# A hybrid RWKV-7 and convolution decoder step on one core: gates, LayerNorm, next input and first loads in another order, and three of each pair's four channel sums as products of two parts

## Chip, core and metric

One Trainium2 chip, one core. The metric is the device time of one execution in microseconds (us). Engines: TensorE (PE in the rows, PEld its weight loads), VectorE (DVE), ScalarE (ACT), GpSimd (POOL) and SyncE (SP), whose queue issues most of the DMAs; ScalarE can issue DMAs too.

## What is computed

One layer, over a prompt of 2048 tokens and 8 single sample tokens, all in float32, with 1024 channels, 16 heads of 64, and a convolution branch of 512 channels. Cut to what matters here:

```python
h = rms_norm(x, norm_pre_g)
proj = h @ w_in                     # r k v z | two lora inputs | conv-glu | z_conv | gate_r gate_c
ps = ps + (ps_prev - ps) * mu_shift # token shift of the first columns
kk = kk * rsqrt(sum(kk * kk, -1) + 1e-12)          # per head (sum 1)
y_w, wkv_new = wkv7_scan(...)                      # recurrence per head
mu = mean(y_w, -1); var = mean(square(y_w - mu), -1)   # GroupNorm per head (sums 2 and 3)
bonus = sum(rh * kh * r_k, -1) * vh                # per head (sum 4)
o_r = (y_gn + bonus) * silu(z_r)
c = causal depthwise conv of width 31 of the GLU
o_c = silu(LayerNorm(c)) * silu(z_c)
merged = sigmoid(g_r) * (o_r @ w_branch_r) + sigmoid(g_c) * (o_c @ w_branch_c)
y = x + rms_norm(merged @ w_out, norm_post_g)
```

## The kernel before

**Tiles and blocks.** Channels lie on the 128 partitions, tokens along the free dimension. The prompt is cut into 4 blocks of 512 tokens (`for b in range(NB)`, L1167). In a block, the 8 pairs of heads are worked on one after the other (`for j in range(HP)`, L1177). `unit_in` (L486) projects r, k, v and z of a pair into "raw" tiles, `unit_a` (L503) makes decay, keys and the triangular solve of the eight 64-token chunks, `unit_b` (L657) runs the recurrence and GroupNorm and leaves the pair's output in an "orr" tile. `unit_in` runs two pairs ahead. Between the pairs, `fill` (L1132) puts in other projections by the strings FILL0 to FILL2 (L299): "u" is `glu` (L743), "n" is `conv_norm` (L762), the LayerNorm of the convolution branch, "z" and "Z" are `conv_gate`, a digit is `gate` (L998), which computes two of the 16 gate tiles and stores them in DRAM. After the pairs come `stage_a` (L376) with the next block's input, its first projections, then eight `merge` steps (L1020), which load the gates again, and `stage_out` (L1045). In the last block `final_states` (L1146) stands ahead of the merge.

**Products.** `gemm` (L307) multiplies float32 values split in two parts: `split` (L137) has ScalarE copy the value into a float32r tile (the high part) and VectorE subtract that from the value (the low part); three products of parts make one product (PASSES, L305), all recorded at L113. The sums over a head's 64 channels go another way: `stat` (L362) is one float32 product of 512 columns with a constant matrix, `ones_b` (ones in two blocks of 64) or `cent` (identity minus the mean). The trace has two records for each such product. A pair has four of them: of the squared keys (L536, stays as it is), of the bonus (L654, input R, output multiplied by V into "keep"), and two of GroupNorm in the "gt" tile (L711 with `cent` into "py", L713 with `ones_b` into "pc").

**Order.** All is unrolled. The framework lays out each engine's instructions ahead of the run by a list scheduler: every instruction has a priority (its place in the program; `tc.high_priority(n)` puts it n places earlier, `later(n)` (L158) n places later), and among what is ready by planned times the earliest goes first. On the chip each engine's queue runs in that fixed order and waits where a semaphore says so. Tiles of one name share a number of buffers (BUFS, L71: x 2, raw 8, orr 8, w 5, ht 8, tmp 4; aw, gd and pz 1 each; "pg" has 3 PSUM banks). `pull` (L725) deals out the convolution's taps on VectorE, the tile "et".

**Lines that the steps touch.** `gate` computes Exp, Ln, Exp on ScalarE in an "x" tile and stores both halves from SP (L1011); `merge` loads them from SP (L1027, L1028) into "x"; `stage_a` loads the next block's input from SP (L385) into "x", scales it on VectorE and splits it into "ht"; `final_states` collects the state in "x"; `stage_first` (L390) loads sample rows on ScalarE's queue and the first block's input on SP's, into "orr" and "x"; L237 loads the convolution weights. P (L662) has a tile "pz"; `pr` (L581), where the solve keeps its products, is in "gd".

Of the kernel before, what the change touches and what calls it, by code (L numbers as in the profile page):

```python
# [18 lines left out]
LN = 60  # L19
# [7 lines left out]
def rwkv7_conformer_step(  # L27
# [91 lines left out]
    def f32(ap):  # L119
        return ap.bitcast(F32)  # L120
# [48 lines left out]
    def cmem(shape, v, name):  # L169
        t = const.tile(shape, F32, name=name)  # L170
        nc.gpsimd.memset(t, v)
        return t
# [5 lines left out]
    ones_b = cmem([128, 128], 0.0, "ones_b")  # L178
# [22 lines left out]
    cent = const.tile([128, 128], F32, name="cent")  # L201
# [3 lines left out]
    stt(cent, ones_b, -1.0 / 64, ident, ALU.mult, ALU.add)  # L205
# [25 lines left out]
    for name, _, n in _VECS:  # L231
# [5 lines left out]
    nc.scalar.dma_start(out=crow[0:NTAP * CT, :], in_=conv_w)  # L237
    ps = pa()
    nc.tensor.transpose(out=ps[:, 0:nrow], in_=rows[0:nrow, :], identity=ident[0:nrow, 0:nrow])
    nc.tensor.transpose(out=ps[:, 128:128 + NTAP * CT], in_=crow[0:NTAP * CT, :],  # L240
                        identity=ident[0:NTAP * CT, 0:NTAP * CT])
    prm = const.tile([128, nrow], F32, name="prm")
    cw = const.tile([128, NTAP * CT], F32, name="cw")
    vcp(prm, ps[:, 0:nrow])
    vcp(cw, ps[:, 128:128 + NTAP * CT])
# [120 lines left out]


# [8 lines left out]
    def stage_a(b):  # L376
# [3 lines left out]
        for k2 in range(KT // 2):  # L380
            xt = new([128, 2, BS], "x")
            for i in range(2):
                with tc.high_priority(HPA):
                    kt = 2 * k2 + i
                    nc.sync.dma_start(out=xt[:, i], in_=x_cols[kt, :, b * BS:b * BS + BS])  # L385
                    stt(xt[:, i], xt[:, i], pv("npre", kt), rb, ALU.mult, ALU.mult)
                    split(ht[kt][:, 0], ht[kt][:, 1], xt[:, i])
        return ht

    def stage_first():  # L390

        n1 = NS + 1
        xs = new([128, D], "orr")
        nc.scalar.dma_start(out=xs[0:NS], in_=x_sample[:, 0, :])
        nc.scalar.dma_start(out=xs[NS:n1], in_=x_prompt[0, T - 1:T, :])
        gb = new([128, D], "orr")
        nc.scalar.dma_start(out=gb[0:n1], in_=norm_pre_g[0:1, :].to_broadcast([n1, D]))
        sh = new([128, D], "orr")
        nc.scalar.dma_start(out=sh[0:NS], in_=state_shift[0])
        xts = [new([128, 2, BS], tag) for tag in ("orr", "orr", "x", "x")]  # L400
        xts = [xts[kt // 2][:, kt % 2] for kt in range(KT)]
        for kt in range(KT):
            nc.sync.dma_start(out=xts[kt], in_=x_cols[kt, :, 0:BS])
# [594 lines left out]
    def gate(b, ht, i0):  # L998
# [11 lines left out]
        for i in range(2):  # L1010
            nc.sync.dma_start(out=gates[b][i0 + i], in_=s[:, i])  # L1011
# [262 lines left out]
```

## Time and profile before

| | |
|---|---|
| median of 3 runs | 2840.21 us (2840.06 to 2844.37) |
| the profiled execution, its own time | 2840.91 us |
| its span, first to last instruction | 2839.0 us |
| mean granted TensorE clock | 0.987 |
| TensorE, VectorE, ScalarE busy | 94%, 69%, 47% |
| HBM traffic over the span | 163 GB/s |

A row of the page's busy table gives an engine's busy time, its share of the span and the count of its instructions. A timeline row gives the start, the duration, the engine, the line, the operation, out<-in by the program's tile names, and in brackets how long the engine had idled and what released it. Neighbours of one kind are merged (x36). SPq and ACTq are DMA issues. A product's record overlaps that of the next, so the rate is read from starts. The time of an execution and its span differ by about 2 us.

### The profile page before, as it was taken

The page shows a single profiled execution, that of the slowest core. Times are in us where ns is not written, and L with a number is a line of the kernel's source. Part 1 is how long each engine was busy: PE and PEld are TensorE (multiplying, and loading weights), DVE is VectorE, ACT ScalarE, POOL GpSimd, SP SyncE. Part 2 cuts the span into 40 slices and gives each one's busy share as a digit, 9 for nine tenths or more (in the row PEclk, how much of TensorE's full clock was granted, in tenths as well). Part 3 has the DMA queues.
Part 4 walks back from the last instruction along what each step waited for, and adds up shares of the span by engine and source line. Part 5 has one row for each costly group of instructions (what it writes and reads, how often), then busy time and mean ns, then how long its engine had stood idle before and what let it go on. Part 6 is the DMA issues. An engine that isn't in the chain of part 4 may idle for free.

```text
span 2839.0 us, 55943 instructions
## 1 busy us (share of the span) xinstructions
PE 2681.9 (94%) x22800; PEld 2127.1 (75%) x22800; DVE 1965.4 (69%) x4560; ACT 1320.4 (47%) x2783; POOL 16.1 (1%) x61
## 2 busy tenths in 40 slices
PE   6999898999999989998999998998999997999988
PEld 6888887888877767776887776776797765767767
DVE  5788798686976667677568667776575767765512
ACT  5555557652334564554023556445312455545411
POOL 0000000000000000000000000000000000000000
PEclk9999999999999999999999999999999999999999
DMA  6545654457863343254665345334565422333474
GB/s 227 185 174 174 207 178 145 160 194 273 293 244 126 104 130 130 96 169 154 227 230 194 103 131 129 115 131 152 163 236 209 149 91 67 121 111 97 136 265 161
DMA packets 157717, 466.92 MB, mean 164 GB/s; under 512 B 19794, under 2 KB 25155, under 8 KB 157452
## 3 DMA queue, kind: packets, MB, share of 16 engines
q1 hardware_dynamic: 154909, 454.23, 48.2%
q10 hardware_dynamic: 2550, 9.12, 0.8%
q8 instruction: 179, 2.93, 0.4%
q14 instruction: 79, 0.64, 0.1%
HBM read 350.41 MB, written 113.35 MB: 163 GB/s over the span
## 4 chain that ended last, share of the span: by engine, by line
PE 52%; DVE 27%; ACT 13%; DMA 4%; issue 3%; SPq 0%; POOL 0%; DVEq 0%; ACTq 0%; POOLq 0%
PE pg L113 35%; PE pa L113 7%; DVE gd L101 5%; DVE zr L605 5%; PE pc L113 4%; PE py L113 4%; DVE zr L107 3%; DVE et L107 3%; ACT sc L95 2%; PE pb L113 2%; DVE raw L107 2%; ACT tmp L95 2%; ACT zbuf L95 2%; DVE w L101 1%; ACT xv L95 1%
## 5 line engine op out<-in xcount | busy, mean ns | idle before, releaser
L113 PE MATMUL pg<-ht,w 128*128 128x512 f32 (+1 forms) x7200 | 1525.0, 363 | 27.5 <-ACT ht L95 14.7
L113 PEld LDWEIGHTS pg<-ht,w 128*128 128x128 f32 x7200 | 1166.1, 189 | 270.5 <-issue 63.1
L107 DVE SCALAR_TENSOR_TENSOR et<-u,cw,et 128x512 f32<-128x512 f32 x480 | 359.3, 748 | 6.6
L95 ACT ACTIVATE raw<-pg,omm 128x512 f32<-128x512 f32 (+1 forms) x155 | 93.0, 603 | 216.0 <-PE pg L113 210.1
L95 ACT ACTIVATE tmp<-tmp 128x512 f32<-128x512 f32 (+1 forms) x305 | 184.7, 625 | 7.4 <-DVE tmp L526 2.4
L101 DVE TENSOR_TENSOR gd<-zr,gp 128x8 f32<-128x8 f32 (+14 forms) x480 | 179.6, 374 | 12.1
L113 PE MATMUL pg<-orr,w 128*128 128x512 f32 (+2 forms) x960 | 186.5, 350 | 1.3 <-ACT orr L95 1.0
L605 DVE TENSOR_REDUCE zr<-gd 128x2 f32<-128x8 f32 (+14 forms) x480 | 176.5, 368 | 11.8
L113 PEld LDWEIGHTS pg<-orr,w 128*128 128x128 f32 x960 | 155.3, 188 | 27.8 <-ACT orr L95 1.4
L95 ACT ACTIVATE w<-wraw 128x512 fp32r<-128x512 f32 x162 | 101.2, 628 | 126.9 <-PE pg L113 80.7
L698 DVE TENSOR_SCALAR xs<-pc,dk 128x64 f32<-128x64 f32 x224 | 63.5, 283 | 107.4 <-PE pc L113 106.1
L107 DVE SCALAR_TENSOR_TENSOR raw<-pg,prm,raw 128x511 f32<-128x511 f32 (+1 forms) x185 | 104.2, 574 | 43.8 <-ACT raw L95 43.3
L101 DVE TENSOR_TENSOR w<-wraw,w 128x512 fp32r<-128x512 f32 x162 | 110.8, 686 | 32.6 <-ACT w L95 32.0
L107 DVE SCALAR_TENSOR_TENSOR zr<-zr,sub 128x5 f32<-128x5 f32 (+7 forms) x512 | 115.7, 226 | 13.3
L95 ACT ACTIVATE sc<-pa 64x256 f32<-64x256 f32 (+1 forms) x192 | 72.9, 380 | 101.2 <-PE pb L113 97.9
L95 ACT ACTIVATE gd<-sc 32x128 f32<-32x128 f32 x256 | 78.4, 306 | 84.2 <-DVE sc L101 81.4
L113 PE MATMUL pa<-ar,bk 64*64 64x128 f32 x2048 | 104.1, 283 | 10.3 <-DVE bk L101 7.7
L101 DVE TENSOR_TENSOR x<-x,pg 128x512 f32<-128x512 f32 (+1 forms) x80 | 45.9, 577 | 97.1 <-PE pg L113 51.3
L113 PEld LDWEIGHTS pa<-ar,bk 64*64 64x64 f32 x2048 | 80.0, 135 | 42.4 <-DVE bk L101 19.4
L101 DVE TENSOR_TENSOR sc<-pa,maskw 128x512 f32<-128x512 f32 x128 | 82.5, 685 | 33.2 <-PE pa L113 33.0
L113 PE MATMUL pg<-xv,w 128*128 128x512 f32 (+2 forms) x320 | 90.5, 356 | 13.2 <-DVE x L101 13.2
L95 ACT ACTIVATE x<-pg 128x512 f32<-128x512 f32 (+1 forms) x80 | 40.8, 510 | 122.2 <-PE pg L113 121.8
(357 smaller groups left out, 3623.9 us busy)
## 6 DMA issues: line engine op xcount, KB each, us to landing
w<-kept_in SPq DMA_DIRECT2D x366, 512.0 KB, 3.3
kept_in<-w SPq DMA_DIRECT2D x122, 512.0 KB, 4.5
wraw<-in_w_in_dram SPq DMA_DIRECT2D x122, 256.0 KB, 3.5
w<-kept_br SPq DMA_DIRECT2D x48, 512.0 KB, 4.3
w<-kept_out SPq DMA_DIRECT2D x40, 512.0 KB, 5.2
gate<-x SPq DMA_DIRECT2D x64, 256.0 KB, 3.7
x<-gate SPq DMA_DIRECT2D x64, 256.0 KB, 3.9
w<-kept_bc SPq DMA_DIRECT2D x24, 512.0 KB, 3.8
```

Source lines behind the costliest of these rows:

```text
L95: return nc.scalar.activation(out=out, in_=in_, func=func, scale=scale, bias=bias, **kw)
L101: return nc.vector.tensor_tensor(out=out, in0=a, in1=b, op=op)
L107: return nc.vector.scalar_tensor_tensor(out=out, in0=a, scalar=s, in1=b, op0=op0, op1=op1)
L113: return nc.tensor.matmul(out=out, lhsT=lhsT, rhs=rhs, start=start, stop=stop, **kw)
L605: nc.vector.tensor_reduce(out=zr[:, 0:n, t:t + 2], in_=pr[:, 0:n, :, 0:w], axis=AX.X, op=ALU.add)
L698: nc.vector.tensor_scalar(out=state[:, j, :] if c == NC - 1 else xs[:, c + 1, :], in0=pu[:, c * C:c * C + C], scalar1=dk[:, c:c + 1], scal ...
```

## The change

- `stat2` is new: it splits its input into the two parts of a new one-buffer tile "st" (`split`: a ScalarE copy, a VectorE subtraction) and adds up two products with the constant matrix, now float32r. It stands in place of `stat` for the bonus sum and the two GroupNorm sums of each pair.
- P moves from its own tile "pz" to "gd".
- `gate` stores both halves in one DMA, from ScalarE's queue; a DRAM tile holds two gates.
- `stage_a` takes "raw" tiles, one for each of the eight loads, in place of two "x" tiles in turn; the final state goes to "aw" in place of "x".
- `conv_norm` is put 200 places later in place of 60.
- The first block's input loads come first on SP, in the order in which they are used; the sample rows follow on SP in place of ScalarE's queue; the convolution weights come 1000 places later, with a transposition of their own.

```diff
--- before.py
+++ after.py
@@ -16,7 +16,7 @@
 RJ = 3
 GE, HPO, HPA = 4, 0, 0
 LI = 1000
-LN = 60
+LN = 200
 HP = 550
 HPW, HPS, HPG, HPU, HPZ = HP, HP, HP, HP, HP
 LN_EXP_SET = 6
@@ -166,16 +166,16 @@
     ident = const.tile([128, 128], F32, name="ident")
     make_identity(nc, ident)
 
-    def cmem(shape, v, name):
-        t = const.tile(shape, F32, name=name)
-        nc.gpsimd.memset(t, v)
+    def cmem(shape, v, name, dt=F32):
+        t = const.tile(shape, dt, name=name)
+        nc.gpsimd.memset(f32(t) if dt == F32R else t, v)
         return t
 
     eps_rms = cmem([128, 1], RMS_EPS, "eps_rms")
     eps_gn = cmem([128, 1], GN_EPS, "eps_gn")
     eps_ln = cmem([128, 1], LN_EPS, "eps_ln")
     eps_kk = cmem([128, 1], 1e-12, "eps_kk")
-    ones_b = cmem([128, 128], 0.0, "ones_b")
+    ones_b = f32(ones_r := cmem([128, 128], 0.0, "ones_b", F32R))
     avg_c = cmem([128, 128], 1.0 / DC, "avg_c")
     rms_d = [dram.tile([4, 128], F32, name=f"rms{b}") for b in range(NB)]
 
@@ -198,11 +198,12 @@
             ctx.enter_context(tc.issue_after(i))
         return ctx
 
-    cent = const.tile([128, 128], F32, name="cent")
+    cent_r = const.tile([128, 128], F32R, name="cent")
     for e in range(2):
         s = slice(e * 64, e * 64 + 64)
         nc.gpsimd.memset(ones_b[s, s], 1.0)
-    stt(cent, ones_b, -1.0 / 64, ident, ALU.mult, ALU.add)
+    stt(cent_r, ones_b, -1.0 / 64, ident, ALU.mult, ALU.add)
+    cent = f32(cent_r)
     id2 = const.tile([128, C], F32, name="id2")
     tt(id2, ident[:, 0:C], ident[:, C:128], ALU.add)
     maskw = cmem([128, 128], 1.0, "maskw")
@@ -234,15 +235,18 @@
     rows = new([128, 128], "sc")
     nc.sync.dma_start(out=rows[0:nrow, :], in_=vecs)
     crow = new([128, 128], "sc")
-    nc.scalar.dma_start(out=crow[0:NTAP * CT, :], in_=conv_w)
+    with later(LI):
+        nc.scalar.dma_start(out=crow[0:NTAP * CT, :], in_=conv_w)
     ps = pa()
     nc.tensor.transpose(out=ps[:, 0:nrow], in_=rows[0:nrow, :], identity=ident[0:nrow, 0:nrow])
-    nc.tensor.transpose(out=ps[:, 128:128 + NTAP * CT], in_=crow[0:NTAP * CT, :],
-                        identity=ident[0:NTAP * CT, 0:NTAP * CT])
     prm = const.tile([128, nrow], F32, name="prm")
+    vcp(prm, ps[:, 0:nrow])
     cw = const.tile([128, NTAP * CT], F32, name="cw")
-    vcp(prm, ps[:, 0:nrow])
-    vcp(cw, ps[:, 128:128 + NTAP * CT])
+    with later(LI):
+        ps = pb()
+        nc.tensor.transpose(out=ps[:, 0:NTAP * CT], in_=crow[0:NTAP * CT, :],
+                            identity=ident[0:NTAP * CT, 0:NTAP * CT])
+        vcp(cw, ps[:, 0:NTAP * CT])
 
     def pv(name, i=None):
         r, n = place[name]
@@ -364,6 +368,15 @@
         mm(ps[:, 0:src.shape[1]], mat, src)
         return ps[:, 0:src.shape[1]]
 
+    def stat2(pool, mat, src):
+
+        parts = new([128, 2, BS], "st", F32R)
+        split(parts[:, 0], parts[:, 1], src)
+        ps = pool()
+        for i in range(2):
+            mm(ps, mat, parts[:, i], start=(i == 0), stop=(i == 1))
+        return ps
+
 
     def rms(src, n, junk_tag, shape):
         junk = new(shape, junk_tag)
@@ -377,30 +390,27 @@
         rb = new([128, BS], "tmp")
         nc.sync.dma_start(out=rb, in_=rms_d[b].rearrange("t p -> (t p)").unsqueeze(0).to_broadcast([128, BS]))
         ht = [new([128, 2, BS], "ht", F32R) for _ in range(KT)]
-        for k2 in range(KT // 2):
-            xt = new([128, 2, BS], "x")
-            for i in range(2):
-                with tc.high_priority(HPA):
-                    kt = 2 * k2 + i
-                    nc.sync.dma_start(out=xt[:, i], in_=x_cols[kt, :, b * BS:b * BS + BS])
-                    stt(xt[:, i], xt[:, i], pv("npre", kt), rb, ALU.mult, ALU.mult)
-                    split(ht[kt][:, 0], ht[kt][:, 1], xt[:, i])
+        for kt in range(KT):
+            xt = new([128, BS], "raw")
+            nc.sync.dma_start(out=xt, in_=x_cols[kt, :, b * BS:b * BS + BS])
+            stt(xt, xt, pv("npre", kt), rb, ALU.mult, ALU.mult)
+            split(ht[kt][:, 0], ht[kt][:, 1], xt)
         return ht
 
     def stage_first():
 
         n1 = NS + 1
-        xs = new([128, D], "orr")
-        nc.scalar.dma_start(out=xs[0:NS], in_=x_sample[:, 0, :])
-        nc.scalar.dma_start(out=xs[NS:n1], in_=x_prompt[0, T - 1:T, :])
-        gb = new([128, D], "orr")
-        nc.scalar.dma_start(out=gb[0:n1], in_=norm_pre_g[0:1, :].to_broadcast([n1, D]))
-        sh = new([128, D], "orr")
-        nc.scalar.dma_start(out=sh[0:NS], in_=state_shift[0])
-        xts = [new([128, 2, BS], tag) for tag in ("orr", "orr", "x", "x")]
+        xts = [new([128, 2, BS], tag) for tag in ("x", "x", "orr", "orr")]
         xts = [xts[kt // 2][:, kt % 2] for kt in range(KT)]
         for kt in range(KT):
             nc.sync.dma_start(out=xts[kt], in_=x_cols[kt, :, 0:BS])
+        xs = new([128, D], "orr")
+        nc.sync.dma_start(out=xs[0:NS], in_=x_sample[:, 0, :])
+        nc.sync.dma_start(out=xs[NS:n1], in_=x_prompt[0, T - 1:T, :])
+        gb = new([128, D], "orr")
+        nc.sync.dma_start(out=gb[0:n1], in_=norm_pre_g[0:1, :].to_broadcast([n1, D]))
+        sh = new([128, D], "orr")
+        nc.sync.dma_start(out=sh[0:NS], in_=state_shift[0])
         rstd = rms(xs, n1, "orr", [128, D])
         h9 = new([128, D], "orr")
         stt(h9[0:n1], xs[0:n1], rstd[0:n1], gb[0:n1], ALU.mult, ALU.mult)
@@ -651,7 +661,7 @@
                 cp(W[hf][es, :, 1, 0:64], psv[ES[1 - e], :, 1, :])
 
         bonv = new([128, BS], "keep")
-        mul(bonv, stat(pa, ones_b, R), V)
+        mul(bonv, stat2(pa, ones_r, R), V)
         return W, ar, aw, xv, zv, dk, bonv, sz
 
     def unit_b(b, j, parts):
@@ -659,7 +669,7 @@
         W, ar, aw, xv, zv, dk, bonv, sz = parts
         pull(UT)
 
-        P = new([128, NC, C], "pz")
+        P = new([128, NC, C], "gd")
         for hf in range(2):
             ps = pa()
             for i in range(4):
@@ -708,9 +718,9 @@
 
         ys = new([128, BS], "gt")
         cp(ys, yps)
-        pcen = stat(pyt, cent, ys)
+        pcen = stat2(pyt, cent_r, ys)
         act(ys, pcen, AF.Square)
-        rsqrt(ys, stat(pct, ones_b, ys), eps_gn, scale=1.0 / 64)
+        rsqrt(ys, stat2(pct, ones_r, ys), eps_gn, scale=1.0 / 64)
         mul(ys, pcen, ys)
         stt(ys, ys, pv("gng", j), bonv, ALU.mult, ALU.add)
         stt(ys, ys, pv("gnb", j), sz, ALU.add, ALU.mult)
@@ -993,7 +1003,7 @@
         mul(oc_s, c, t)
 
     G0 = N_SHIFT + 3 * DC
-    gates = [[dram.tile([128, BS], F32, name=f"gate{b}_{i}") for i in range(2 * KT)] for b in range(NB)]
+    gates = [[dram.tile([128, 2, BS], F32, name=f"gate{b}_{i}") for i in range(KT)] for b in range(NB)]
 
     def gate(b, ht, i0):
 
@@ -1007,8 +1017,7 @@
                     vcp(gate_s[:, i0 + i, :], v.s[0])
         act(s, s, AF.Ln, bias=1.0)
         act(s, s, AF.Exp, scale=-1.0)
-        for i in range(2):
-            nc.sync.dma_start(out=gates[b][i0 + i], in_=s[:, i])
+        nc.scalar.dma_start(out=gates[b][i0 // 2], in_=s)
 
     def merge_prep(b, orr):
         if b == SB:
@@ -1024,8 +1033,8 @@
                         (w_branch_c[m], ("bc", m), lambda kt, part: oc[kt][part], w2)])
         sc = new([128, 2, BS], "x")
         s, c = sc[:, 0], sc[:, 1]
-        nc.sync.dma_start(out=s, in_=gates[b][m])
-        nc.sync.dma_start(out=c, in_=gates[b][KT + m])
+        nc.sync.dma_start(out=s, in_=gates[b][m // 2][:, m % 2])
+        nc.sync.dma_start(out=c, in_=gates[b][(KT + m) // 2][:, m % 2])
         for t, v in ((s, br), (c, bcv)):
             for ps, sl in v.parts:
                 mul(t[:, sl], t[:, sl], ps)
@@ -1144,7 +1153,7 @@
             gate(b, ht, 2 * int(what))
 
     def final_states():
-        sf = new([64, HP, 2, 64], "x")
+        sf = new([64, HP, 2, 64], "aw")
         for e, es in enumerate(ES):
             ps = pb()
             for h in range(HP):
```

## Rows read from the trace of the kernel before

**Rows 1.** The page: busy times of the engines, and the chain by engine.

```profile
PE 2681.9 (94%) x22800; PEld 2127.1 (75%) x22800; DVE 1965.4 (69%) x4560; ACT 1320.4 (47%) x2783; POOL 16.1 (1%) x61
...
PE 52%; DVE 27%; ACT 13%; DMA 4%; issue 3%; SPq 0%; POOL 0%; DVEq 0%; ACTq 0%; POOLq 0%
```

**Rows 2.** Windows: span, busy PE, PEld, DVE, ACT, POOL (count), clock, DMA, GB/s.

```profile
127.50:435.00 307.50, 294.11 (x3173) 261.67 (x3172) 267.71 (x660) 175.12 (x376) 1.35 (x4) 0.99 0.55 180
...
1500.00:2038.00 538.00, 510.36 (x4594) 380.16 (x4593) 368.29 (x907) 274.78 (x579) 2.70 (x8) 0.99 0.43 136
2038.00:2200.00 162.00, 160.19 (x969) 137.54 (x968) 109.62 (x214) 30.95 (x82) 0.00 (x0) 1.00 0.61 209
```

**Rows 3.** Timeline, block 2: a stream of projections, and two sums.

```profile
1845.10 24.63 PE L113 MATMUL pg<-ht,w 128*128 128x512 f32 x105
...
1892.12 1.02 PE L113 MATMUL pc<-gt,ones_b 128*128 128x512 f32 x2
...
1892.98 1.02 PE L113 MATMUL pa<-tmp,ones_b 128*128 128x512 f32 x2
```

**Rows 4.** The tile ones_b: durations, ns min/median/max, first and last start.

```profile
L113 PE MATMUL pa<-raw,ones_b x64: 592/697/1222, 110.7 to 2666.5; 128*128 128x512 f32 x64
```

**Rows 5.** Timeline, block 2: a bonus sum, and what follows it.

```profile
1873.50 1.13 PE L113 MATMUL pa<-raw,ones_b 128*128 128x512 f32 x2 [0.49 <-ACT sc L95]
...
1874.56 0.42 PEld L556 LDWEIGHTS pb<-ident,raw 128*128 128x128 f32 x4 [0.76 <-ACT zbuf L95]
...
1874.66 0.69 DVE L101 TENSOR_TENSOR keep<-pa,raw 128x512 f32<-128x512 f32 x1 [4.17 <-PE pa L113]
```

**Rows 6.** Timeline, block 2: the split of a pair's output.

```profile
1897.40 0.63 ACT L95 ACTIVATE orr<-gt 128x512 fp32r<-128x512 f32 x1
...
1898.62 0.68 DVE L101 TENSOR_TENSOR orr<-gt,orr 128x512 fp32r<-128x512 f32 x1
```

**Rows 7.** Timeline, the last block's variance sum to its second merge step.

```profile
2685.22 16.80 PE L113 MATMUL pg<-ht,w 128*128 128x512 f32 x70
...
2704.14 1.04 ACT L95 ACTIVATE x<-x 128x1024 f32<-128x1024 f32 x1
...
2719.79 0.86 SPq L1011 DMA_DIRECT2D gate<-x  x2
...
2728.03 0.33 SPq L1027 DMA_DIRECT2D x<-gate  x1
...
2731.62 0.80 PE L113 MATMUL pg<-xv,w 128*128 128x512 f32 x1 [12.75 <-DVE x L101]
```

**Rows 8.** Windows (columns as in rows 2) behind two idle times of TensorE.

```profile
2731.60:2737.00 5.40, 5.38 (x13) 4.22 (x14) 2.55 (x4) 0.63 (x1) 0.00 (x0) 0.50 0.39 137
...
1720.80:1726.00 5.20, 5.18 (x10) 3.49 (x11) 5.20 (x15) 1.32 (x2) 0.00 (x0) 0.50 0.51 49
```

**Rows 9.** Timeline of the start: a DMA issued by ScalarE.

```profile
17.80 0.28 ACTq L409 DMA_DIRECT2D out_dram<-orr  x1
```

**Rows 10.** Timeline: TensorE's waits for the next block's input.

```profile
1294.96 0.72 PE L113 MATMUL pg<-ht,w 128*128 128x512 f32 x2 [3.15 <-ACT ht L95]
...
1307.68 2.39 PE L113 MATMUL pg<-ht,w 128*128 128x512 f32 x9 [2.21 <-ACT ht L95]
...
1976.84 0.73 PE L113 MATMUL pg<-ht,w 128*128 128x512 f32 x2 [2.26 <-ACT ht L95]
...
1985.05 1.81 PE L113 MATMUL pg<-ht,w 128*128 128x512 f32 x5 [3.26 <-ACT ht L95]
```

**Rows 11.** Waits of SP's queue: us in total, times, longest us.

```profile
SPq L385 <- DMA gate<-x: 8.6, 4, 3.7
```

**Rows 12.** Waits of TensorE: us in total, times, longest us.

```profile
PE pg L113 <- DVE tmp L101: 18.2, 5, 7.4
```

**Rows 13.** Timeline of the start: the first sum and the first projection.

```profile
20.71 2.05 PE L113 MATMUL py<-tmp,avg_c 128*128 128x512 f32 x2 [4.38 <-DVE tmp L101]
...
25.64 1.03 PE L113 MATMUL pg<-ht,w 128*128 128x264 f32 x3 [2.88 <-ACT ht L95]
```

## The prediction

> **What bounds the kernel now.** I read the page's busy table and its chain first. TensorE is busy 94% of the span and holds 52% of the chain; VectorE has 69% and 27% [rows 1]. Next the windows by stage. In the merge of block 2 (2038 to 2200 us) TensorE is busy 160.2 of 162 us; in the pair stage of that block 510.4 of 538 us with VectorE at 368; in block 0, where the weights are also split, VectorE is busy 267.7 of 307.5 us (87%) beside TensorE's 294.1 [rows 2]. So TensorE sets the pace nearly everywhere, VectorE comes close in block 0, and the page's 6% of idle TensorE, 157 us, is the most that mere reordering could give. A change gains either by giving TensorE less to do or by closing one of its few long waits. This one tries both. The profiled execution took 2840.9 us (span 2839.0), 0.7 above the median of the runs, 2840.2; I sum against the first and take 0.7 off at the end.
>
> **The sums as two products.** One sum is two TensorE passes now. Between the start of the GroupNorm sum and that of the sum behind it lie 0.86 us, while a projection product of the same 512 columns takes 24.63/105 = 0.235 us in a stream [rows 3]. Two such products take 0.47, so a sum in the stream gets 0.39 us cheaper. Of the three sums of a pair, two (the centring and the variance) stand in that stream: 64 x 0.39 = 25 us.
>
> The bonus sum stands elsewhere. It has 64 records, two for each of the 32 pairs [rows 4], and one takes 1.06 us from its start to the next product, which had itself waited 0.76 us for a ScalarE copy [rows 5]. If it alone held TensorE up, 0.59 x 32 = 19 us would go; if that copy ends last anyway, nothing. I take 7, nearer to nothing, because the row shows the copy as what released the next product. Sum: 32 us off, bounds 25 and 44.
>
> **What the splits cost.** Each sum gets a ScalarE copy of 0.63 us and a VectorE subtraction of 0.68 us like those of the existing split of the pair's output [rows 6]: 96 x 0.63 = 60 us of ScalarE, 96 x 0.68 = 65 us of VectorE. The bonus sum's split has cover: its input is ready before VectorE's long solve, and VectorE idles 4.17 us for that sum today [rows 5]. The two of GroupNorm lengthen its serial tail by 2 x 1.31 = 2.6 us a pair, less 0.8 saved in the sums. What hides this is that nothing reads that tail's result before the merge, while TensorE has projections queued; but ScalarE and VectorE are in order, and the next pair's gate and key work (the inputs of its solve) stands behind these four instructions. If all of it came onto the path: 64 x 1.31 = 84 us. If none, 0. I take 6, about one subtraction (0.68) for each of the eight pairs of block 0, where VectorE has least room. The single "st" buffer orders the three splits of a pair, whose uses lie several us apart already, and P in the "gd" buffer comes between the solve that last reads it and the next pair's that refills it: both at nothing; without that distance the next solve would start later by the wait for P's products.
>
> **Gates.** At the end of the last block ScalarE finishes a gate at 2705.18 (2704.14 + 1.04), but SP issues its stores only at 2719.79, behind weight loads that wait for buffers. The merge can then load its gates only at 2728.03, and TensorE idles 12.75 us, to 2731.62 [rows 7]. After that it runs 5.4 us at a granted clock of 0.50, the 1.2 GHz level, with 13 products where 23 fit at the full clock: 5.4 - 13 x 0.235 = 2.3 us more [rows 8]. Issued by ScalarE right behind its own Exp, the store lands some 14 us sooner; and the final states, moved to "aw", free the second "x" buffer. Prize 15 us; nothing at worst. I take 14, since the loads that follow stay in SP's queue. The Trainium skill ("DMA: Bandwidth & Descriptors", section on issuing engines not being separate DMA queues) says that issuing from another engine saves only the sequencer's time to issue. By that rule this term would be two issues of under half a microsecond instead of 14, and the sum about 14 us smaller. The row speaks against it here: what delays the store is its place in SP's in-order queue, not its transfer.
>
> Elsewhere the 32 stores on ScalarE cost about 0.28 us each [rows 9], 9 us on an engine busy 47%: nothing. SP loses 64 issues, which brings weight loads forward, if anything.
>
> **Next input.** Its eight loads go through the two "x" buffers, which gates also hold. TensorE waits for the split input 2.26 and 3.26 us before block 3, and 3.15 and 2.21 us before block 2 [rows 10]: 10.9 us. SP waits for gate stores before these loads [rows 11]. With the eight "raw" buffers, four free since the pair before last, the first four loads can be issued early. Bounds 0 and 11. I take 8: the normalisation and the split stay, as does the wait for the "ht" buffers that the last projections free.
>
> **LayerNorm.** TensorE waits 18.2 us in five pieces, the longest 7.4, for the sums that VectorE prepares [rows 12]; after one of them the clock is again at 0.50 for 5.2 us with 10 products, a loss of 5.2 - 10 x 0.235 = 2.9 us [rows 8]. The variance sum sits in TensorE's order just behind the mean, while VectorE still subtracts and squares. Moving LayerNorm from 60 to 200 places later lets more projection work stand ahead, but the order is laid out by planned times, and VectorE may still be late. All of it would be 18.2 + about 6 of clock = 24; at worst the longest wait arises once more, -7.4. I take 9, half of the waits.
>
> **First loads.** The first sum waits 4.38 us for VectorE and the first projection 2.88 us for the input [rows 13]. The x loads now go out ahead of weights and sample rows, in the order in which they are used; the weights and the sample rows come later. At most 7.3 us, at worst minus 3. I take 3. The convolution weights, put off, are needed only by the taps much later: nothing.
>
> **Sum.** 32 - 6 + 14 + 8 + 9 + 3 = 60 us. 2840.9 - 60 = 2781, by the median 2780.
>
> **The rivals.**
> (a) The pair's chain sets the pace, not TensorE: the passes taken off turn into waits for the solve. For it: VectorE's 27% of the chain [rows 1] and the waits around the bonus sum [rows 5]. Against it: behind the last pair's variance sum TensorE still has 70 projection products queued, 16.8 us [rows 7], so its work, not the chain, ends the stage. The time: only 14 + 8 + 9 + 3 = 34 us come off less 6, 2812. The Trainium skill ("Perfetto Trace Analysis", Identifying the Most-Contended Engine) says that matmul busy share is no good measure and weight-load busy share is a better one. By that rule TensorE would have a quarter of room (75% on the page) and this rival would be the forecast; the waits in the stage windows speak for TensorE.
> (b) The waits come back elsewhere: the merge's gate loads stay behind weight loads on SP, and the variance sum is again early. Then 14 and 9 are lost from the sum: 2803.
> (c) Slower: the two GroupNorm splits of each pair go on the path in full, because the next pair's inputs stand behind them on ScalarE and VectorE. Price 84 us, less the 25 of the passes if they lie on that chain, less the 34 of the waits: +25, 2865. It decides from the point where the queue of projections at the end of a block is used up: 16.8 us over eight pairs, 2.1 us a pair. The passes already eat about 0.8 to 1 us of these, so a chain longer by over about 1.2 us a pair does it. My 6 us stay below that.
>
> **How the numbers follow.** Forecast 0.58; (a) 0.19; (b) 0.15; (c) 0.05; about no change 0.03. The time is the forecast's, 2780. Its own best end has 44 + 15 + 11 + 24 + 7 = 101 us off and no split cost, 2739; its poor end is 25 - 6 + 10 = 29 off, 2811, which also covers (a) and (b). The range 2744 to 2816 leaves out (c), no change, and the farthest end where all terms come out best at once. A measurement tells about 0.2% (5.7 us) from no change. Faster: forecast, (a) and (b), 0.92; same 0.03; slower 0.05.
>
> **What would show it.** Right: the two records of each changed GroupNorm sum 0.24 us apart; TensorE's busy time down by about 30 us; the 12.75 us gap before the second merge step gone, no stretch at clock 0.50 behind it, and gate stores on ScalarE's queue just after the Exp; waits of "pg" for VectorE's "tmp" well under 18 us; input waits before blocks 2 and 3 under 2 us. Wrong: TensorE's busy time falls but its idle time grows by as much, with longer waits before the solve's products or the first key products (rival a or c); VectorE over 95% in block 0; or the gap of the last merge still there, only elsewhere (b).

## The result and the profile after

The changed kernel takes 2859.2 us against 2842.5 for the kernel before on the same chip: ratio 1.0059, 95% interval 1.0043 to 1.0075. It is slower by 0.6%; forecast were 2780 us and a range of 2744 to 2816. The profiled execution has a span of 2854.5 us, 15.5 more than before.

The page after, its busy table, its clock line and the engines' shares of the chain [rows 1]:

```profile
span 2854.5 us, 56188 instructions
...
PE 2673.5 (94%) x22800; PEld 2153.2 (75%) x22800; DVE 2014.2 (71%) x4656; ACT 1361.2 (48%) x2879; POOL 16.1 (1%) x61
...
PE 55%; DVE 27%; ACT 12%; issue 3%; DMA 2%; SPq 0%; POOL 0%; DVEq 0%; ACTq 0%; POOLq 0%
```

VectorE and ScalarE gained 49 and 41 us with 96 instructions more each; counted were 65 and 60 as a sum of durations, while the busy time counts a moment in which two records overlap only once. TensorE's busy time fell by 8 us only, not by 30, and its idle time (span less busy) grew from 157 to 181 us. The waits of TensorE for others, after (each: us in total, how often, the longest) [rows 12]:

```profile
PE pa L113 <- DVE bk L101: 41.4, 15, 5.8
PE pb L113 <- DVE gd L619: 26.3, 21, 6.3
PE pa L424 <- DVE orr L107: 14.4, 1, 14.4
...
PE pg L113 <- DVE x L101: 8.5, 1, 8.5
...
PE pg L113 <- ACT ht L95: 7.2, 3, 3.3
...
PE pg L113 <- DVE tmp L101: 1.2, 2, 0.9
```

and the same lines before:

```profile
PE pb L113 <- DVE gd L609: 18.9, 18, 4.8
PE pg L113 <- DVE tmp L101: 18.2, 5, 7.4
PE pg L113 <- ACT ht L95: 14.7, 6, 3.3
PE pg L113 <- DVE x L101: 13.2, 2, 12.8
PE pa L414 <- DVE orr L107: 10.2, 1, 10.2
...
PE pa L113 <- DVE bk L101: 7.7, 5, 5.5
```

The waits that the change aimed at are shorter: LayerNorm's sums (tmp) 18.2 to 1.2, the next input (ht) 14.7 to 7.2, the last merge's gates (x) 13.2 to 8.5. In their place stands the wait for a pair's keys, bk: 7.7 to 41.4.

**Where along the run.** The first product with keys (pa<-ar,bk) marks a block's start; in the timeline, block 1 of the changed kernel begins at

```profile
842.88 0.44 PE L113 MATMUL pa<-ar,bk 64*64 64x128 f32 x4
```

Read so for each kernel, the time from the start of a block's keys to that of the next (the first column is all before block 0, the last runs to the end):

| us | start | block 0 | block 1 | block 2 | block 3 and end |
|---|---|---|---|---|---|
| before | 76.3 | 745.3 | 693.2 | 701.4 | 622.8 |
| after | 81.5 | 761.4 | 702.1 | 691.3 | 618.2 |
| orders alone (e2) | 81.2 | 752.5 | 694.9 | 690.9 | 623.5 |
| sums alone (e1) | 76.6 | 764.5 | 702.3 | 699.2 | 618.9 |
| orders and bonus sum (e11) | 82.1 | 746.9 | 685.2 | 686.9 | 619.5 |

Blocks 2 and 3 gained 15 us together. The start lost 5, block 0 lost 16 and block 1 lost 9.

### The profile page after: what moved, and what is told of

It is laid out like the page before. It is cut to its first block, busy times and chain, and to the rows that moved or that the text cites. A ratio compares the mean times of both kernels' runs of the same rounds, so it can differ in the third digit from the quotient of the medians.

```text
span 2854.5 us, 56188 instructions
## 1 busy us (share of the span) xinstructions
PE 2673.5 (94%) x22800; PEld 2153.2 (75%) x22800; DVE 2014.2 (71%) x4656; ACT 1361.2 (48%) x2879; POOL 16.1 (1%) x61
## 4 chain that ended last, share of the span: by engine, by line
PE 55%; DVE 27%; ACT 12%; issue 3%; DMA 2%; SPq 0%; POOL 0%; DVEq 0%; ACTq 0%; POOLq 0%
PE pg L113 35%; PE pa L113 9%; DVE zr L615 5%; DVE gd L101 5%; PE pc L113 4%; PE py L113 4%; DVE zr L107 3%; ACT sc L95 2%; PE pb L113 2%; DVE et L107 2%; DVE raw L107 2%; ACT tmp L95 2%; ACT zbuf L95 2%; DVE w L101 1%; DVE sc L101 1%
## 5 line engine op out<-in xcount | busy, mean ns | idle before, releaser
L113 PE MATMUL pg<-ht,w 128*128 128x512 f32 (+1 forms) x7200 | 1501.2, 359 | 16.8 <-ACT ht L95 7.2
L113 PE MATMUL pa<-ar,bk 64*64 64x128 f32 x2048 | 114.9, 312 | 48.3 <-DVE bk L101 41.4
L113 PEld LDWEIGHTS pa<-ar,bk 64*64 64x64 f32 x2048 | 87.7, 151 | 85.5 <-DVE bk L101 56.8
L101 DVE TENSOR_TENSOR keep<-pa,raw 128x512 f32<-128x512 f32 x32 | 22.1, 692 | 103.8 <-PE pa L113 103.8
```

The source lines that it names most:

```text
L101: return nc.vector.tensor_tensor(out=out, in0=a, in1=b, op=op)
L113: return nc.tensor.matmul(out=out, lhsT=lhsT, rhs=rhs, start=start, stop=stop, **kw)
```

## The experiments

The theories that the expectations name: **A**, the two GroupNorm splits stand on in-order ScalarE and VectorE on the way to the next pair's keys; **B**, the lighter or reordered stream lets projections run ahead, so that none is left to cover the key work; **C**, it is LayerNorm at 200 places; **D**, it is the half clock after short waits.

**The change in two halves.**

```diff
e1:  before, with stat2 for the three sums and P in "gd"; all orders as before
e2:  after, with   mul(bonv, stat(pa, ones_b, R), V),   pcen = stat(pyt, cent, ys),   stat(pct, ones_b, ys)
```

> The kernel before with the three sums in two parts (and P in gd, so that the new tile fits), all else as before. Theory A (the splits stand on the way to the next pair's keys: ScalarE and VectorE do them in order ahead of the key work): slower than before, by 10 us or more (2852 or above), with TensorE's waits for VectorE's bk well above the 7.7 us of before (30 us or more). Theory B (the reordered queues let projections run ahead, so that none is left beside the key work): the sums alone save what was forecast, 2805 to 2825, waits for bk as before. Theory C (LayerNorm 200 places later does it): as B.

> The changed kernel with the three sums as single float32 products again; the new orders of gates, LayerNorm, next input and first loads stay. Theory A: faster than before, 2805 to 2825, waits of TensorE for bk about 8 us. Theory B: slower than before, 2850 or above, waits for bk 30 us or more. Theory C: as B.

Measured: the sums alone 2864.1 us, ratio 1.0070 (1.0046 to 1.0095), with the bk wait at 39.7 us in 15 pieces; the orders alone 2842.9, 0.9996 (0.9983 to 1.0008), with 7.3 in 7. So the sums carry the whole loss and the key waits, and the orders gain nothing. For e2 that is neither A's range nor B's: A foresaw a gain, B a loss.

**Two of the orders undone in the changed kernel.**

```diff
e3:
-LN = 200
+LN = 60
e4:
-        nc.scalar.dma_start(out=gates[b][i0 // 2], in_=s)
+        for i in range(2):
+            nc.sync.dma_start(out=gates[b][i0 // 2][:, i], in_=s[:, i])
```

> The changed kernel with LayerNorm 60 places later in place of 200. Theory C: at least 15 us faster than the changed kernel (2844 or below), the waits for bk in the pair after each LayerNorm gone. Theories A and B: within 8 us of the changed kernel, or slower by the waits for the variance sum that come back (18 us on the page of before).

> The changed kernel with the gates stored by SP in two DMAs as before (the DRAM layout stays). Theory B in its narrow form (ScalarE's stores free the x buffers sooner, so that gate projections run ahead): at least 8 us faster than the changed kernel in the pairs, of which the last merge gives some back. Theories A and C: within 5 us of the changed kernel in the pairs; at the last merge the wait for the gates is as long as before (about 12 us against 8.5), so 0 to 8 us slower in all.

Measured: 2857.1 us, ratio 1.0053 (1.0034 to 1.0071), and 2853.8, 1.0037 (1.0026 to 1.0048). C falls, and so does B in its narrow form, which wanted e4 at least 8 us faster than the changed kernel (2859.2). The gate stores are no better on ScalarE's queue than on SP's.

**Which sums.**

```diff
e5, before with:
+        pcen = stat2(pyt, cent_r, ys)
+        rsqrt(ys, stat2(pct, ones_r, ys), eps_gn, scale=1.0 / 64)
e6, before with:
+        mul(bonv, stat2(pa, ones_r, R), V)
```

> The kernel before with only the two GroupNorm sums of each pair as two products of parts (P in gd); the bonus sum stays one float32 product. Theory A (the two splits stand on ScalarE and VectorE ahead of the next pair's key work): nearly all of the loss seen with all three sums is here, 2855 to 2866 us, and TensorE waits over 30 us for VectorE's bk. Theory B (any cheaper sum lets the projections run ahead, so that none is left beside the key work): about two thirds of the loss, 2853 to 2858, bk waits 20 to 30 us.

> The kernel before with only the bonus sum of each pair as two products of parts (P in gd). Theory A: its split has cover, so no loss and a gain of 0 to 10 us, 2833 to 2843, bk waits as before, under 10 us. Theory B: a third of the loss, 2848 to 2852, bk waits 12 to 20 us.

Measured: GroupNorm's two 2854.4 us, ratio 1.0050 (1.0030 to 1.0070); the bonus sum 2830.7, 0.9958 (0.9945 to 0.9972). The bonus sum gains, and the loss is GroupNorm's. By its time e5 lies just below A's range and in B's. The bk waits do not follow A's numbers (17.9 and 22.6 us): they grew in the kernel that got faster too. A wait at that place is thus a poor measure of the loss.

**The split's price taken apart.** All four start from the kernel before with P in "gd" (that move alone was not run). e7 has no split at all: the instruction that makes a sum's input writes it rounded, and one product (stat1) stands for the sum. e14 does so for GroupNorm's two sums alone. e9 keeps ScalarE's copy of those two. e10 keeps both parts but subtracts on GpSimd.

```diff
e14:
+        yr = new([128, BS], "st", F32R)
+        cp(yr, yps)
+        pcen = stat1(pyt, cent_r, yr)
+        act(yr, pcen, AF.Square)
+        rsqrt(ys, stat1(pct, ones_r, yr), eps_gn, scale=1.0 / 64)
e7:  e14, and R written rounded for stat1 in the bonus sum
e9:  e5 with   cp(parts[:, 0], src)   and one product
e10: e5 with   nc.gpsimd.tensor_tensor(out=parts[:, 1], in0=src, in1=f32(parts[:, 0]), op=ALU.subtract)
```

> The kernel before with each of the three sums as a single product of its input rounded once, written so by the instruction that makes it: no split, no subtraction; it leaves out the low parts of the three sums. TensorE's work falls by more than in the changed kernel (three of four passes of each of 96 sums) and nothing is added to ScalarE and VectorE. Theory A: it is the splits that cost, so this one is faster than before by 30 to 60 us, 2783 to 2813, bk waits under 8 us. Theory B: it is TensorE's lighter stream that leaves no cover, so no faster than before, 2843 to 2865, with bk waits of 25 us or more. Theory D (the loss is the half clock that follows each short wait): stretches at clock 0.50 as long as in the changed kernel, and no gain.

> As the kernel with only the two GroupNorm sums in parts, but with ScalarE's rounded copy alone and one product: VectorE's subtraction and the second product are left out, and with them the low part of both sums. Measured so far: both parts 2854, no split at all (all three sums rounded) 2815. If it is the subtraction, for which VectorE stands idle until ScalarE's copy is there (57 us in all in the kernel with both parts), that costs: 2815 to 2832, and VectorE's idle time ahead of st gone. If ScalarE's copy in the tail costs as much as the subtraction: 2833 to 2848. If neither, the loss is in TensorE's order: 2848 or more.

> The two GroupNorm sums as single products of inputs written rounded, no split at all, the bonus sum as before; it leaves out the low part of both sums. Beside the kernel with ScalarE's copy (2839) and the one with copy and subtraction (2854) it gives the price of the 64 copies. If the copy is cheap: 2832 to 2840, so passes taken from TensorE are worth little here. If the copy costs like the subtraction: 2815 to 2828.

> As the kernel with only the two GroupNorm sums in parts, with the subtraction of the low part on GpSimd, which is busy 1% of the span, instead of VectorE; nothing is left out. If the cost is the place that the subtraction takes in VectorE's in-order queue: 2822 to 2842, bk waits under 12 us. If it is the length of the tail itself, on whatever engine: 2852 or more, since GpSimd is likely slower than 0.69 us at it.

Measured: e7 2814.7 us, ratio 0.9908 (0.9888 to 0.9929); e14 2829.0, 0.9946 (0.9930 to 0.9962); e9 2838.7, 0.9980 (0.9969 to 0.9992); e10 2880.9, 1.0127 (1.0110 to 1.0145). e7 misses A's range by 2 us, e9 fits a copy as dear as the subtraction, e14 lies between its two ranges. The ratios of e14, e9 and e5 give a ladder for the 64 GroupNorm sums, in us of 2842 (each step is uncertain by some 6 us):

- No split, one product: -15.3 (interval -20 to -11). On TensorE 64 x (0.86 - 0.235) = 40 us went [rows 3], so a pass taken off is worth 38% of its time, 27 to 50% by the interval.
- With ScalarE's copy: -5.7. 64 copies of 0.62 us cost 9.7, 0.15 each.
- With subtraction and second product: +14.2, which is 19.9 more. The second product, priced at 38% like the others (an estimate), is 64 x 0.235 x 0.38 = 6; the subtraction takes the other 14, 0.22 each.

B falls as the main cause: e7 and e14 have the lightest streams and are faster. D falls as a cause by itself: e14 has a mean clock of 0.975 and e5 0.973, and they lie 25 us apart. In e10 the subtraction is out of VectorE's queue, but takes twice the time, and TensorE now stands waiting for it; the tile's operations and TensorE's waits there:

```profile
L95 ACT ACTIVATE st<-gt x64: 612/622/635, 128.5 to 2735.2; 128x512 fp32r<-128x512 f32 x64
L373 POOL TENSOR_TENSOR st<-gt,st x64: 1263/1289/1776, 129.2 to 2735.9; 128x512 fp32r<-128x512 f32 x64
```

```profile
PE pc L113 <- POOL st L373: 12.0, 23, 1.0
...
PE py L113 <- POOL st L373: 8.9, 18, 0.9
```

These waits are 21 us, and the bk waits are no shorter than in e5 (20.1 against 17.9). So the tail's length counts, not only its place on VectorE: the sums have their places in TensorE's fixed order. The run is not clean, though: some of VectorE's own instructions become longer beside GpSimd's. The convolution's taps in e10, and in e5:

```profile
L107 DVE SCALAR_TENSOR_TENSOR et<-u,cw,et x480: 708/749/1765, 158.0 to 2275.9; 128x512 f32<-128x512 f32 x160
...
L107 DVE SCALAR_TENSOR_TENSOR et<-u,cw,et x480: 709/748/755, 157.0 to 2254.3; 128x512 f32<-128x512 f32 x160
```

VectorE is busy for 1981.6 us in e10 and 1962.4 in e9, with 4560 instructions in both. How much of the 22 us between e10 and e5 this is was not taken apart.

**The tail elsewhere in the queues.**

```diff
e8, after: what follows cp(ys, yps) in unit_b is issued from unit_a of the next pair
+        last = mul(bk[:, :, 1, :], c3(K), c3(em))
+        if tail:
+            with behind(act_last.ins, last.ins):
+                orr.append(tail())
```

> The changed kernel with GroupNorm's tail of a pair (both splits, sums and what follows) queued on ScalarE and VectorE behind the instructions that make the next pair's keys. Theory A: the keys come out about 3 us a pair sooner, bk waits fall from 41 us to under 12 and the time to 2815 to 2840; if the tail then delays the mask and solve on VectorE, 2840 to 2855 with new waits behind sc or bk. Theory B: the order of TensorE's stream sets it, bk waits over 25 us, 2850 to 2862.

Measured: 2864.9 us, ratio 1.0092 (1.0072 to 1.0112), above all three ranges and no faster than the changed kernel; the bk waits fall to 17.4 us, between A's 12 and B's 25. The keys do come sooner: in block 2, from the second pair's recurrence (its first pc<-xs,aw) to the third's first key product, 17.0 us in place of 20.1. But from the second pair's keys to the solve's first product (pb<-gd,sc) it is 31.7 in place of 28.0. What the tail gave up ahead of the keys it took behind them. A has to be put more widely: in both places where it was tried, ahead of the next pair's keys and behind them, the tail costs about the same.

**Does the shared buffer tie the splits?** Alone the two halves of the sums gave +14 and -12 us, together +20.

```diff
e13, e1 with:
+        pcen = stat2(pyt, cent_r, ys, "gp")
+        rsqrt(ys, stat2(pct, ones_r, ys, "gp"), eps_gn, scale=1.0 / 64)
```

> The kernel before with all three sums in parts, as in the first experiment, but GroupNorm's parts in the solve's buffer gp, which is free at that time, so that they share no buffer with the bonus sum's parts in st. Alone, the two GroupNorm sums measured +14 us and the bonus sum -10, together +21 where they should add to +4. If the shared buffer is what ties them: 2838 to 2850, and the pairs of block 0 no longer slower from key products to solve. If the splits crowd VectorE and ScalarE whatever the buffer: 2856 or more.

Measured: 2861.1 us, ratio 1.0061 (1.0047 to 1.0075). The shared "st" was rightly put at nothing. The table of blocks leads to block 0. One of its stretches, from the third pair's (j = 2) first key product to its solve's first product, by engine, before:

```profile
core 0: us, PE busy (x) PEld busy (x) DVE busy (x) ACT busy (x) POOL busy (x), PEclk, DMA share, GB/s
214.10:254.10 40.00, 38.71 (x394) 36.77 (x393) 37.28 (x103) 17.67 (x36) 0.17 (x1) 1.00 0.62 211
```

and after:

```profile
225.00:272.60 47.60, 45.71 (x457) 44.02 (x458) 47.53 (x124) 20.63 (x41) 0.00 (x0) 1.00 0.69 228
```

VectorE is busy for 47.53 of 47.60 us and has 124 instructions in place of 103. The timeline of VectorE at the beginning of that stretch, after:

```profile
224.75 0.69 DVE L101 TENSOR_TENSOR gt<-py,gt 128x512 f32<-128x512 f32 x1
...
225.95 0.75 DVE L107 SCALAR_TENSOR_TENSOR gt<-gt,prm,keep 128x512 f32<-128x512 f32 x1
...
227.21 0.75 DVE L107 SCALAR_TENSOR_TENSOR gt<-gt,prm,keep 128x512 f32<-128x512 f32 x1
...
229.14 0.69 DVE L101 TENSOR_TENSOR orr<-gt,orr 128x512 fp32r<-128x512 f32 x1
...
232.08 0.68 DVE L101 TENSOR_TENSOR st<-raw,st 128x512 fp32r<-128x512 f32 x1
```

GroupNorm's tail of the pair before and the bonus split stand here among weight splits and convolution taps, and the solve waits its turn. In the kernel before, the tail's last instruction (orr) starts ahead of the first key product:

```profile
212.46 0.68 DVE L101 TENSOR_TENSOR orr<-gt,orr 128x512 fp32r<-128x512 f32 x1
...
214.14 0.44 PE L113 MATMUL pa<-ar,bk 64*64 64x128 f32 x4
```

In the changed kernel it starts at 229.14, 4 us behind it. The five instructions shown take 3.6 us; more of the stretch is filled by the convolution. The same two windows for the tile "et" alone, before and after:

```profile
214.10:254.10 40.00, 9.52 (x13) 0.00 (x0) 1.00 0.62 211
...
225.00:272.60 47.60, 16.36 (x23) 0.00 (x0) 1.00 0.69 228
```

Ten more of the convolution's operations, 6.8 us, stand ahead of the solve's first product: the planner laid out another order. Of the pairs of block 0, counted from 0, pairs 1, 2 and 4 take 47 to 48 us over this stretch in e1, e13 and after, and 39 to 42 before and in e5, e6 and e17. Two kernels take the parts out of block 0 alone:

```diff
e16, after with:
+        mul(bonv, (stat2(pa, ones_r, R) if b else stat(pa, ones_b, R)), V)
e16 and e17, after with:
+        pcen = stat2(pyt, cent_r, ys) if b else stat(pyt, cent, ys)
+        rsqrt(ys, stat2(pct, ones_r, ys) if b else stat(pct, ones_b, ys), eps_gn, scale=1.0 / 64)
```

> The changed kernel with all three sums as float32 products in block 0, where VectorE also splits the weights, and in parts in blocks 1 to 3. In the profiles so far block 0 (from its first key product to that of block 1) takes 745.3 us before, 752.5 with the orders alone, 761.4 in the changed kernel. If the crowding of VectorE in block 0 is the greater part of the loss: block 0 at 750 to 754 and the time 2846 to 2853. If what block 0 gives up is lost again later: 2855 or more.

> The same with only the two GroupNorm sums as float32 products in block 0; the bonus sum is in parts everywhere. Block 0 took 746.9 us in the kernel with the new orders and the bonus sum in parts. If GroupNorm's splits are what lengthens block 0: block 0 at 746 to 752 and the time 2841 to 2849, still 15 to 23 us above that kernel (2826), as much as the splits cost in blocks 1 to 3. If the bonus sum's split crowds block 0 as well: 2850 or more.

Measured: 2843.3 us, ratio 1.0002 (0.9991 to 1.0013), and 2840.2, 0.9991 (0.9980 to 1.0001); block 0 takes 751.6 and 749.6 us; the blocks are as expected, the times 1 to 3 us below their ranges. Relieving block 0 of GroupNorm's parts gives back all that the changed kernel lost against before. The same stretch of the same pair in e17:

```profile
222.40:262.40 40.00, 37.91 (x390) 35.94 (x390) 37.60 (x105) 18.20 (x37) 0.18 (x1) 1.00 0.66 217
```

VectorE has 2.4 us to spare there, 15 operations of "et" in place of 23, and the stretch is 40 us long again. e17 is still 0.58% (16 us) above e11 below: what GroupNorm's parts cost in blocks 1 to 3. By the profiles 11.8 us of it lie in block 1 (697.0 us, and 685.2 in e11), and there ahead of the keys, where theory A put them: from the recurrence of pairs 1 to 4 (first pc<-xs,aw) to the next pair's first key product it is 22.1, 22.7, 21.2 and 23.1 us in e17, and 18.5, 19.6, 19.6 and 20.9 in e11. The pushed solve of block 0 is not the whole cost either: e5 does not have it and loses 6.0 us in block 0 and 9.1 in block 1 (profiles of before and e5); where these go was not tried.

**A version that beats both.**

```diff
e11: after with   pcen = stat(pyt, cent, ys)   and   stat(pct, ones_b, ys)
e12: e11 with LN = 60 and the first loads as before
e15: e12 with the centring sum split straight from PSUM
+        split(yp[:, 0], yp[:, 1], yps)
...
+        for i in range(2):
+            mm(pcen, cent_r, yp[:, i], start=(i == 0), stop=(i == 1))
```

> The changed kernel with the two GroupNorm sums back as float32 products: the new orders and the bonus sum in parts. If the parts add up as measured alone (orders 0, bonus sum -10): 2825 to 2835, ratio 0.994 to 0.998. If the lighter bonus sum spoils the new orders as the three sums together did: 2838 or more.

> The bonus sum in parts with only the gate stores, the final states' buffer and the next input of the changed kernel: LayerNorm at 60 places and the first loads as before. If the first loads cost the 3 to 5 us that the start shows (VectorE's wait of TensorE 10.2 us before, 13.4 with the orders alone): 2 to 6 us below the kernel with all orders and the bonus sum, 2820 to 2832. If LayerNorm's place was worth something, that much slower: 2832 to 2845.

> The kernel with the bonus sum in parts, the gate stores and the next input (2822 us), and the centring sum in parts too, split straight from PSUM: the rounded copy takes the place of the present copy, so only VectorE's subtraction is added to the tail; the variance sum stays one float32 product. Saved on TensorE 32 x 0.39 = 12.5 us, added on VectorE 32 x 0.69 = 22 us. If a tail split costs what the measurements so far make of it (about half a us each beyond the passes): 2822 to 2832. If without ScalarE's second copy the subtraction is cheap: 2812 to 2820.

Measured: e11 2825.7 us, ratio 0.9933 (0.9917 to 0.9948); e12 2821.8, 0.9920 (0.9905 to 0.9936); e15 2823.9, 0.9924 (0.9907 to 0.9941). e12 is the lowest of the kernels that leave nothing out, 0.8% below the kernel before, though e11 and e15 lie within its noise: the bonus sum in parts, the gate stores on ScalarE, the final state in "aw" and the next input in "raw". Its first key product comes at 76.7 us, that of e11 at 82.1. With one copy fewer in the tail, the centring sum in parts (e15) shows neither gain nor loss.

## Why the prediction was wrong, step by step

**GroupNorm's splits: the step that failed.** The prediction put them at 6 us between bounds of 0 and 84, because "nothing reads that tail's result before the merge, while TensorE has projections queued". That is true of the result, not of the engines. By the ladder the splits cost 24 us (9.7 for copies, 14 for subtractions) where GroupNorm's sums alone are in parts; in the changed kernel, beside the new orders and the bonus split, the sums in parts cost 1.0059 - 0.9933 = 1.26%, 36 us, and with the 10 us that their passes were worth the splits are, by estimate, at 46. The place named, block 0, was half of it: against e11 the changed kernel loses 14.5 us in block 0 and 16.9 in block 1. The size, "about one subtraction (0.68) for each of the eight pairs", was wrong: VectorE had 2.7 us to spare in the 40 us from keys to solve, and once it was full the solve came some 8 us later in three pairs.

**The passes: the second failed step.** 25 us were counted for GroupNorm's sums, as if TensorE set the pace. The ladder gives 38% of that. Rival (a) saw this. The rule of the Trainium skill that it cited ("Perfetto Trace Analysis", section "Identifying the Most-Contended Engine": weight-load share as the better measure of how full TensorE is) fits better, with 75% on the profile's page, than the busy share of 94% on which the prediction relied. That the chain of a pair bounds much of the pair stage is the reading that fits e14; it was not shown pair by pair. Nor do the two products of a changed sum stand 0.24 us apart, as the signs had it: the first starts on the copy, the second waits for the subtraction. After:

```profile
1047.71 0.50 PE L113 MATMUL py<-st,cent 128*128 128x512 f32 x1 [1.20 <-ACT st L95]
1048.44 0.72 PE L113 MATMUL py<-st,cent 128*128 128x512 f32 x1 [0.23 <-DVE st L101]
```

**Rival (c)** had the sign and, by 6 us, the time (2865), with a chance of 0.05. That time is luck: its terms of 84 us for the splits, 25 for the passes and 34 for the waits were all too large and cancelled. Its point of decision, a chain longer by over 1.2 us a pair, lay below the 2.6 us that the prediction itself had worked out for the splits, and below the 1.8 that are left of them when the sums' 0.8 is taken off. Its place was half right: behind the keys (e8) the tail costs the same. The cushion that it named, projections left at a block's end, does not decide: from the start of block 1's last recurrence to block 2's first key product it is 176.6 us after and 186.3 before, from block 2 to 3 192.3 and 217.7, but e12, which is faster than before, has 175.2 and 192.0.

**The bonus sum**: 7 taken, 12 measured (e6). The row read was the right one, and the gain fits the reason given, that the split has cover; the price of this split was not taken apart.

**Next input**: 8 taken; the waits for ht fell by 7.5, from 14.7 to 7.2 [rows 10]. That the number fits is partly luck: without this order they are 10.4 in e1, 5.6 in e6 and 5.1 in e14, with it 3.2 in e2 and 9.6 in e4. Together with the gates it did pay beside the bonus sum: e12 lies 0.38% (11 us) under e6, where 22 had been taken for the two.

**Gates**: 14 taken; at most 4 came. TensorE's wait in the last merge fell from 12.75 [rows 7] to 8.46 us, but it is 9.7 with the stores back on SP (e4) and 9.4 in e1, where all orders are as before. The store now follows the Exp at once, which ends at 2726.24:

```profile
2726.28 0.33 ACTq L1020 DMA_DIRECT2D gate<-x  x1
```

Yet TensorE waits, and behind the wait its granted clock is 0.50 as before [rows 8]:

```profile
2748.00:2751.50 3.50, 3.17 (x8) 2.49 (x9) 2.86 (x5) 0.63 (x1) 0.00 (x0) 0.50 0.04 15
```

The timeline of SP's queue there, after:

```profile
2739.91 0.32 SPq L149 DMA_DIRECT2D w<-kept_br  x1
2740.33 0.66 SPq L1162 DMA_DIRECT2D out_dram<-aw  x1
2741.09 0.70 SPq L1168 DMA_DIRECT2D out_dram<-tmp  x1
2741.83 0.83 SPq L1036 DMA_DIRECT2D x<-gate  x1
```

and of TensorE:

```profile
2738.79 1.09 PE L113 MATMUL pg<-orr,w 128*128 128x512 f32 x4
2748.33 0.79 PE L113 MATMUL pg<-xv,w 128*128 128x512 f32 x1 [8.46 <-DVE x L101]
```

The loads are late now: they stand on SP behind weight loads that wait for buffers, and behind the final state. That is rival (b) at this place. "The loads that follow stay in SP's queue" took one us off the prize of 15, and it is the wait itself. The Trainium skill ("DMA: Bandwidth & Descriptors", issuing engines are not separate DMA queues) would have put this term near nothing; e4, with the stores back on SP, is no slower (ratio 1.0037 against 1.0059).

**LayerNorm**: 9 taken. The waits went (18.2 to 1.2) in the changed kernel, but not in the kernel with the orders alone (23.0), and 60 places do as well as 200 (e3). So the place in the program does not decide this wait; what does was not tried.

**First loads**: 3 taken, -3 the worst bound; 4 to 5 us were lost. TensorE's first sum, after [rows 13]:

```profile
18.88 1.87 PE L424 MATMUL pa<-ident,orr 8*128 8x8 f32 x16 [14.38 <-DVE orr L107]
25.12 2.05 PE L113 MATMUL py<-tmp,avg_c 128*128 128x512 f32 x2 [4.38 <-DVE tmp L101]
```

The two waits that were to go are as long as before (4.38 and 2.89); what stands ahead of them, the sample rows put behind the x loads, comes 4.4 us later. The first of the two rows before (the second was at 20.71):

```profile
14.46 1.87 PE L414 MATMUL pa<-ident,orr 8*128 8x8 f32 x16 [10.18 <-DVE orr L107]
```

The prediction priced the waits and not the work in front of them.

**The orders together**: 34 taken, 0 measured (e2). By the profiles block 2, which holds the loads for block 3, gains 10.5 us, the start loses 4.9 and block 0 loses 7.2. Why block 0 loses those 7 with the orders alone was not tried.

## What to carry to other kernels

Work taken off the busiest engine is worth its time only where that engine sets the pace; try it by a kernel that drops the work and adds nothing (e14), and price the replacement by adding one instruction at a time (e9, e5). A result that nobody needs soon still occupies in-order queues: look at what stands behind each added instruction in the fullest stretch of that engine, not at its share of the span. Where a change consists of parts, run each alone: here the bonus sum, the gate stores and the next input were together worth 0.8%, and the two GroupNorm sums took more than that away.

## What was not expected of the hardware

TensorE's granted clock falls around waits of a few microseconds and stays low beyond them. In the changed kernel, between 1045 and 1061 us TensorE works little (GroupNorm's and LayerNorm's sums, then 5.77 us of waiting for keys). Three stretches around it, after:

```profile
1040.00:1050.00 10.00, 7.73 (x73) 4.44 (x71) 4.85 (x13) 7.18 (x14) 0.00 (x0) 0.93 0.32 100
1060.50:1072.00 11.50, 8.33 (x88) 5.70 (x90) 9.24 (x16) 9.47 (x24) 0.00 (x0) 0.50 0.00 1
1073.00:1085.00 12.00, 11.93 (x69) 9.54 (x64) 10.16 (x39) 11.21 (x22) 0.00 (x0) 1.00 0.65 24
```

The key products of that pair all run at 0.50, the 1.2 GHz level. The mean granted clock is 0.987 before and 0.969 after. If every lower clock is at the half level, that is 2 x 0.013 = 2.6% of the span before and 6.2% after, some 74 and 177 us, and at most half of the difference, 51 us, is lost work. It can explain why TensorE's busy time fell by 8 us only. It is no cause of its own, since the faster e14 has 0.975: the low clock comes with the waits and makes them cost more than their length, a term that the prediction had counted only for the gates and LayerNorm.

VectorE's instructions can become longer beside GpSimd's: beside the subtractions (1289 ns each) a tap of VectorE took up to 1765 ns, where without them none took over 755 (e10 and e5).
